# Left-factor remainders of an MLP matrix, made by ScalarE's negation and an accumulating transfer in 64 of 112 steps

## The chip, the cores and the metric

The kernel runs as one program on one core of a Trainium2 chip. The core has five engines that run side by side: TensorE (PE in the profile; its weight loads are PEld), VectorE (DVE), ScalarE (ACT), GpSimd (POOL) and SyncE (SP), which here only issues transfers. Sixteen DMA engines move data between the chip's memory (DRAM) and the core's on-chip memory (SBUF). Matmuls write to PSUM banks. The metric is the device time of one execution, in microseconds (us), median of three runs.

## The reference, cut to what matters

One layer of a diffusion backbone over 1024 tokens of width 1024, in fp32: a modulated RMSNorm, a convolution mixer and an mLSTM mixer, a merge and an output projection, and then an MLP with a squared ReLU. The change touches only the MLP's second matrix and the loads for the residual:

```python
def ffn(h, w1, w2):
    return jnp.square(jax.nn.relu(h @ w1)) @ w2
...
x = x + g1 * out
x = x + g2 * ffn(modulate(x, norm2_w[l], sh2, sc2), w_ff1[l], w_ff2[l])
...
return rmsnorm(x, final_norm_w)
```

`w_ff1` is 1024 x 4096 and `w_ff2` is 4096 x 1024. The result of the last line is the kernel's output.

## The kernel before, in words

**Precision.** Every large product is made from fp32 numbers that are cut in two. `split` has ScalarE write `hi`, the number in the matmul's rounded fp32r format, and VectorE write `lo = src - hi`, the remainder. A product then takes three matmul passes (`PASS`): hi by hi, hi by lo, lo by hi. In the third pass the left factor's `lo` is the weight that TensorE loads.

**The second matrix.** It is computed as seven products of half-size blocks (Strassen-Winograd), in the order m = 1, 5, 2, 6, 7, 3, 4. Each product has 512 tokens by 512 output columns, and its inner dimension of 2048 is walked in 16 steps k of 128, so that there are 7 x 16 = 112 steps (`steps`). One step is 4 token tiles x 3 passes = 12 matmuls of 128x512. For m = 4 the last token tile is cut in pieces of 288 and 224 columns. The last 4 steps of m = 4 are run tile by tile at the very end, with each tile's epilogue (gate, residual sum, RMSNorm, store) behind it.

**What a step needs.** The left factor is a 128x512 block of the squared-ReLU features or of a sum of their quarters. The first matrix's stage stores these to DRAM (`fq`) on POOL's queue. The right factor is a 128x512 block of `w_ff2`, or a sum that VectorE makes from several.

- `gather(i)` has SP load the left block to the left half `L` of a staging tile `wst` (six buffers) and the blocks of `w_ff2`. A right factor lies in the right half `R` of the same `wst` or in a page `wq`.
- `prepare(i)` splits both factors to `whi` and `wlo`, 128x1024 each, left half for the left factor. `ring` gives each of them four buffers, so step i + 4 writes where step i was read.
- `step(i, ...)` issues the 12 matmuls.

**Order.** Instructions of this stage are kept in program order on every engine. In iteration i of the main loop comes `gather(i + 4)`, then `prepare(i + 3)`, then the matmuls of step i, then a piece or two of pending VectorE work (`later`: sums of products in PSUM, gates, residuals). `prepare(i + 3)` overwrites the buffers of step i - 1, so ScalarE waits there until TensorE has finished step i - 1. A step's factors are thus made while TensorE runs the three steps ahead of it.

**How prepare splits before.** For m = 2, 7 and 4 both factors lie side by side in `wst` and are split as one 128x1024 piece. For m = 1, 5, 6 and 3 each half is split for itself, 128x512. `load_rows` loads the residual rows (eight tiles `x` of 512 KB, from `x1s` in DRAM): four at once at the start of m = 2, four at once within m = 6. `page` takes a 4 KB-per-partition buffer from a pool of 37; `keep` pins an instruction in program order.

Of the kernel before, what the change touches and what calls it, by code (L numbers as in the profile page):

```python
# [7 lines left out]
F32 = mybir.dt.float32  # L8
F32R = mybir.dt.float32r
AF = mybir.ActivationFunctionType  # L10
ALU = mybir.AluOpType
# [49 lines left out]
def tile_block(ctx: ExitStack, tc: tile.TileContext, x, cx, w_mod1, w_mod, w_v0, w_v, w_unit, w_conv, w_mls, w_o, w_f1, w_f2, cols_d, rows_d, cst_d, out):  # L61
    nc = tc.nc
# [19 lines left out]
    V, A, G, PE, SY = Engine(nc.vector), Engine(nc.scalar), Engine(nc.gpsimd), Engine(nc.tensor), nc.sync  # L82
# [10 lines left out]
    def dma(dst, src, pin=True):  # L93
        i = SY.dma_start(dst, src)
        if pin:
            tc.keep_in_program_order(i)
# [7 lines left out]
    def page(shape, dt=F32, name="pg"):  # L104
        return pg.tile(shape, dt, tag="pg", name=nm(name))
# [21 lines left out]
    def split(src, hi, lo, eng_hi=None, eng_lo=None, pin=False):  # L127
        p, pinned[0] = pinned[0], pinned[0] or pin
        V.tensor_copy(hi, src) if eng_hi is V else A.activation(hi, src, AF.Copy)
        (eng_lo or G).tensor_tensor(lo, src, hi.bitcast(F32), op=ALU.subtract)  # L130
        pinned[0] = p

    def load_w_now(src, eng_lo=None, eng_hi=None):
        n = 1024
        st = ws.tile([P, n], F32, tag="wst", name=nm("wst"))
        dma(st, src, pin=False)
        hi = ws.tile([P, n], F32R, tag="whi", name=nm("whi"))
        lo = ws.tile([P, n], F32R, tag="wlo", name=nm("wlo"))
        split(st, hi, lo, eng_hi, eng_lo)
        return hi, lo  # L140
# [32 lines left out]
    def keep(f):  # L173


        def call(*a, **kw):
            p, pinned[0] = pinned[0], True
            f(*a, **kw)
            pinned[0] = p

        return call
# [41 lines left out]
    def wide(st, eng_hi=None, eng_lo=None):  # L223
        hi, lo = page([P, 1024], F32R, "whi"), page([P, 1024], F32R, "wlo")
        split(st, hi, lo, eng_hi, eng_lo, pin=True)
        return hi, lo
# [573 lines left out]
    L, R = slice(0, 512), slice(512, 1024)  # L800
# [25 lines left out]
    def quads(name, n):  # L826

        return [dpool.tile([n, P, w], F32, name=f"{name}{i}") for i, w in enumerate((512, 1024, 1024, 1024))]
# [209 lines left out]
    def grow(s, bs):  # L1038
        g = page([P, D], name="grow")
        for hf in range(2):  # L1040
            for k in range(4):
                PE.transpose(bs[hf][:, k * P : (k + 1) * P], m2[:, s, 4 * hf + k : 4 * hf + k + 1].to_broadcast([P, P]), ident)
            A.copy(g[:, hf * 512 : hf * 512 + 512], bs[hf])
        return g
# [186 lines left out]
    def ring(n_, i, dt, n=4):  # L1231

        return home("2" + n_, i, n, lambda s_, d_, _: (in_ws if i % n < 2 else page)(s_, d_, n_), dt)
# [205 lines left out]
    fq = quads("fq", NP)  # L1439
# [128 lines left out]
    SRC = {1: (0, 0), 2: (1, 0), 4: (1, 1), 5: (2, 0), 6: (2, 1), 7: (3, 0), 3: (3, 1)}  # L1568
# [14 lines left out]
    steps = [(m, k) for m in (1, 5, 2, 6, 7, 3, 4) for k in range(NP)]  # L1583
    sums2, made2 = {}, {}

    def gather(i):

        m, k = steps[i]
        st = ring("wst", i, F32, 6)
        t_, h_ = SRC[m]  # L1590
        dma(st[:, L], fq[t_][k][:, h_ * 512 : h_ * 512 + 512])
        b = st[:, R]
        if m == 1:
            quarter(0, k)
            b = wblock(0, k)
        elif m == 5:
            quarter(1, k, b)
            V.tensor_tensor(wblock(0, k), b, wblock(0, k), op=ALU.subtract)
            b = wblock(0, k)
        elif m == 2:  # L1600
            quarter(2, k, b)
        elif m == 6:
            quarter(3, k)
            V.tensor_tensor(wblock(0, k), wblock(3, k), wblock(0, k), op=ALU.subtract)
            b = wblock(0, k)
        elif m == 7:
            quarter(1, k, b)
            V.tensor_tensor(b, wblock(3, k), b, op=ALU.subtract)
        elif m == 3:
            b = wblock(3, k)  # L1610
        else:
            quarter(2, k, b)
            V.tensor_tensor(b, b, wblock(0, k), op=ALU.subtract)
        sums2[i] = st, b

    def prepare(i):
        m, k = steps[i]
        st, b = sums2.pop(i)
        hi, lo = ring("whi", i, F32R), ring("wlo", i, F32R)
        if m in (2, 7, 4):  # L1620
            split(st, hi, lo, eng_lo=V)
        else:
            split(st[:, L], hi[:, L], lo[:, L], eng_lo=V)
            split(b, hi[:, R], lo[:, R], eng_lo=V)
        made2[i] = hi, lo

    def step(i, ts, o, more):
        m, k = steps[i]
        ab = made2[i]
        for j in ts:  # L1630
            for n_, (a, b) in enumerate(PASS):
                keep(PE.matmul)(o[j], ab[a][:, j * P : (j + 1) * P], ab[b][:, R], start=not more and k == 0 and n_ == 0, stop=k == NP - 1 and n_ == 2, skip_group_check=True)
# [5 lines left out]
    def last_tile(i, c):  # L1638
        m, k = steps[i]
        ab = made2[i]  # L1640
        cols_ = slice(512, 512 + CUT) if c == 0 else slice(512 + CUT, 1024)
        for n_, (a, b) in enumerate(PASS):
            keep(PE.matmul)(last_banks[c], ab[a][:, 3 * P : 4 * P], ab[b][:, cols_], start=k == 0 and n_ == 0, stop=k == NP - 1 and n_ == 2, skip_group_check=True)

    AHEAD = 3
    def four(name):
        t = [page2([P, 2, 512], name=name) for _ in range(2)]
        return [t[j // 2][:, j % 2, :] for j in range(4)]

    def gated_sum(t, s, o, u=None):  # L1650

        tmp = []

        def first():
            tmp.append(half("ftmp"))
            V.tensor_tensor(tmp[0], o, u if u is not None else g2[:, s], op=ALU.add if u is not None else ALU.mult)

        steps_ = [first]
        if u is not None:
            steps_.append(lambda: V.tensor_tensor(tmp[0], tmp[0], g2[:, s], op=ALU.mult))  # L1660
        steps_.append(lambda: V.tensor_tensor(x1[t][:, s], x1[t][:, s], tmp[0], op=ALU.add))
        return steps_

    def load_rows(ts):
        for t in ts:
            x1[t] = page([P, D], name="x1")
            dma(x1[t], x1s[t])
# [7 lines left out]
    def first_steps():  # L1675
# [2 lines left out]
            prepare(i)  # L1678
        gather(AHEAD)

    fp.steady(fe, first_steps)
    fp.end_d(NP - 1)

    LAST = 4
    tail = len(steps) - LAST
    assert not later
    for i in range(tail):
        m, k = steps[i]
        if i + AHEAD + 1 < len(steps):
            gather(i + AHEAD + 1)  # L1690
        prepare(i + AHEAD)
        o = Y if m in (5, 6, 3) else X
        if m == 4:
            step(i, range(3), o, True)
            for c in range(2):
                last_tile(i, c)
        else:
            step(i, range(4), o, m == 2)
        if i == 1:
            fp.post(NP - 1)  # L1700
            ua, ub = four("ua"), four("ub")
        if i == 3:
            g2 = grow(3, Y[0:2])
            fw = page([P, D], name="fw")
            dma(fw, rows_d[0:1, 1056:2080].to_broadcast([P, D]))
        if m == 2 and k == 0:
            load_rows(range(4))
        if m == 6 and k == 8:
            load_rows(range(4, 8))
        for _ in range(2 if m == 3 else 1):  # L1710
            if later:
                later.pop(0)()
        if k == NP - 1:
            assert not later
            if m == 1:
                for j in range(4):
                    A.copy(ua[j], X[j])
            elif m == 5:
                later += [lambda j=j: V.tensor_tensor(ub[j], Y[j], ua[j], op=ALU.add) for j in range(4)]
            elif m == 2:  # L1720
                for j in range(4):
                    later += gated_sum(j, L, X[j])
            elif m == 6:
                later += [lambda u=u, j=j: V.tensor_tensor(u[j], Y[j], u[j], op=ALU.add) for j in range(4) for u in (ua, ub)]
            elif m == 7:
                for j in range(4):
                    later += gated_sum(4 + j, R, X[j], ub[j])
                later += gated_sum(7, L, X[3], ua[3])
                for j in range(3):
                    later += gated_sum(4 + j, L, ua[j])  # L1730
            elif m == 3:
                a, b, c, d = [gated_sum(j, R, Y[j], ub[j]) for j in (2, 3, 0, 1)]
                a.pop(0)()
                b.pop(0)()
                later += a + b + c + d
    prepare(len(steps) - 1)
    for f in later:
        f()
# [124 lines left out]
```

## Time and profile before

| What | Value |
|---|---|
| median of three runs | 1784.93 us (1784.78 to 1785.35) |
| the profiled execution's own time | 1784.66 us |
| its span, first to last instruction | 1782.9 us |
| TensorE busy | 1738.9 us, 98% of the span |
| VectorE busy | 1269.6 us, 71% |
| ScalarE busy | 754.8 us, 42% |
| GpSimd busy | 192.8 us, 11% |
| moved by DMA | 261.11 MB, mean 146 GB/s |

The profile is one execution. All times in it count from the span's start. The span leaves out 1.8 us of the execution's own time, around the first and last instruction. A group's row gives the operation, its output and inputs by the program's names, the shape, a count, the busy time and the mean duration, and then the idle time of the engine just before, with what ended it. Nearly every instruction carries line 75 (a helper that records them), so groups are told apart by the names. A matmul's row of 386 to 390 ns is the time until its last result; the next one starts earlier, so the pace is read from the starts or from counts over a stretch. The second matrix's steps lie between 1450 and 1760 us, and the end of the span is the epilogue of the last four token tiles.

### The profile page before, as it was taken

The numbers are of one execution on the slowest core, as the hardware profiler recorded it, in microseconds if no ns is written. First come the engines' busy times: TensorE is split into PE (matmuls) and PEld (weight loads), VectorE is DVE, ScalarE is ACT, GpSimd is POOL, SyncE is SP. The second block draws the span as 40 slices with busy tenths as digits, with TensorE's granted clock in tenths as the row PEclk, the third lists the DMA queues.
The fourth block names the chain that finished last, engine by engine and source line by source line (L and its number), as shares of the span: only waits on it lengthen the run. The fifth ranks groups of instructions, "written<-read, shape, count | busy, mean of one in ns | idle before, by whom it ended". The sixth has DMA issues, their size and how long they took to land.

```text
span 1782.9 us, 23518 instructions
## 1 busy us (share of the span) xinstructions
PE 1738.9 (98%) x8633; PEld 1433.6 (80%) x8633; DVE 1269.6 (71%) x2224; ACT 754.8 (42%) x1239; POOL 192.8 (11%) x269
## 2 busy tenths in 40 slices
PE   7999999999999999999999999999999999999994
PEld 3898889877878888888888888877888888888884
DVE  5557565564876669878889987877666656577785
ACT  5633544556343332222244435644444354343434
POOL 3202122212300000000000001111011000000001
PEclk9999999999999999999999999999999999999997
DMA  8213131321534452433647255135334285665352
GB/s 325 77 47 91 46 93 43 89 70 61 174 145 142 157 197 97 140 131 124 228 167 284 71 207 183 72 138 187 130 141 178 112 279 194 233 230 199 104 181 94
DMA packets 102108, 261.11 MB, mean 146 GB/s; under 512 B 11624, under 2 KB 24808, under 8 KB 101992
## 3 DMA queue, kind: packets, MB, share of 16 engines
q1 hardware_dynamic: 85672, 200.88, 34.5%
q0 software_dynamic: 16320, 58.73, 8.3%
q8 instruction: 67, 1.10, 0.3%
q14 instruction: 49, 0.40, 0.1%
HBM read 198.62 MB, written 60.95 MB: 146 GB/s over the span
## 4 chain that ended last, share of the span: by engine, by line
PE 65%; DVE 4%; ACT 2%; issue 1%; ACTq 0%; DVEq 0%
PE psg L75 65%; ACT y L75 1%; DVE wlo L75 1%; DVE gate L75 0%; DVE wst L75 0%; ACT Fsh L75 0%; DVE y L75 0%; ACT fc L75 0%; DVE fc L75 0%; DVE Gv L75 0%; DVE x L75 0%; DVE ftmp L75 0%; DVE Ff L75 0%; DVE Fsl L75 0%; DVE u L75 0%
## 5 line engine op out<-in xcount | busy, mean ns | idle before, releaser
L75 DVE TENSOR_TENSOR wlo<-wst,whi 128x512 fp32r<-128x512 f32 (+1 forms) x236 | 223.5, 950 | 144.5 <-ACT whi L75 144.0
L75 ACT ACTIVATE whi<-wst 128x512 fp32r<-128x512 f32 (+1 forms) x238 | 195.8, 826 | 262.4 <-PE psg L75 170.4
L75 PE MATMUL psg<-whi,wlo 128*128 128x512 f32 (+2 forms) x688 | 266.2, 387 | 0.0
L75 PE MATMUL psg<-whi 128*128 128x512 f32 (+2 forms) x688 | 266.2, 387 | 0.0
L75 PE MATMUL psg<-wlo,whi 128*128 128x512 f32 (+2 forms) x688 | 265.7, 386 | 0.1
L75 PE MATMUL psg<-hh,whi 128*128 128x512 f32 x440 | 176.0, 406 | 0.0
L75 PE MATMUL psg<-hh,wlo 128*128 128x512 f32 x440 | 172.7, 398 | 1.3 <-DVE wlo L75 1.3
L75 PE MATMUL psg<-hl,whi 128*128 128x512 f32 x440 | 172.0, 397 | 0.0
L75 PEld LDWEIGHTS psg<-wlo,whi 128*128 128x128 f32 x688 | 129.3, 188 | 28.0 <-DVE wlo L75 0.6
L75 PEld LDWEIGHTS psg<-whi,wlo 128*128 128x128 f32 x688 | 129.2, 188 | 27.3
L75 PEld LDWEIGHTS psg<-whi 128*128 128x128 f32 x688 | 129.2, 188 | 27.0
L75 PEld LDWEIGHTS psg<-hh,wlo 128*128 128x128 f32 x440 | 83.1, 189 | 20.5 <-DVE wlo L75 1.7
L75 PEld LDWEIGHTS psg<-hl,whi 128*128 128x128 f32 x440 | 83.1, 189 | 17.3
L75 PEld LDWEIGHTS psg<-hh,whi 128*128 128x128 f32 x440 | 82.4, 189 | 17.9
L75 PE MATMUL psg<-oh,Fsl 128*128 128x512 f32 x240 | 94.8, 395 | 0.1
L75 PE MATMUL psg<-oh,Fsh 128*128 128x512 f32 x240 | 94.9, 395 | 0.0
L75 PE MATMUL psg<-ol,Fsh 128*128 128x512 f32 x240 | 94.5, 394 | 0.0
L75 DVE TENSOR_TENSOR u<-psg,u 128x512 f32<-128x512 f32 x67 | 45.8, 686 | 51.5 <-PE psg L75 51.5
L75 PE MATMUL psg<-whi,hh 128*128 128x256 f32 (+1 forms) x256 | 76.0, 297 | 0.0
L75 PE MATMUL psg<-wlo,hh 128*128 128x256 f32 (+1 forms) x256 | 73.2, 286 | 0.0
L75 PE MATMUL psg<-whi,hl 128*128 128x256 f32 (+1 forms) x256 | 73.1, 286 | 0.0
L75 POOL TENSOR_TENSOR wqz<-w,q 64x256 f32<-64x256 f32 x64 | 48.9, 768 | 159.1 <-PE pso L75 141.2
(347 smaller groups left out, 3868.3 us busy)
## 6 DMA issues: line engine op xcount, KB each, us to landing
wst<-fq SPq DMA_DIRECT2D x112, 256.0 KB, 2.8
wst<-in_w_unit_dram SPq DMA_DIRECT2D x38, 512.0 KB, 5.2
mst<-in_w_mod_dram SPq DMA_DIRECT2D x32, 512.0 KB, 4.3
fq<-Ff POOLq DMA_DIRECT2D x32, 512.0 KB, 4.2
wst<-in_w_f_dram SPq DMA_DIRECT2D x64, 256.0 KB, 3.1
wst<-in_w_f_dram SPq DMA_DIRECT2D x21, 512.0 KB, 4.3
Hwst<-in_w_unit_dram SPq DMA_DIRECT2D x18, 512.0 KB, 5.2
x<-in_x_dram SPq DMA_DIRECT2D x16, 512.0 KB, 6.0
```

Of the source, the lines that this page charges most:

```text
L75: i = f(*a, **kw)
```

## The change

For m = 5, 6, 7 and 3 (64 of the 112 steps) the left factor's `lo` no longer comes from VectorE. ScalarE writes `hi` as before and then `-hi` to `lo`, and a transfer issued from POOL's queue adds the left block from DRAM to `lo`, so that `lo = -hi + src`. The block is still loaded to `wst` as well, since `hi` is made from it. The right factor is split by ScalarE and VectorE as before, but now always as a piece of its own, so that m = 2 and m = 4 split two 128x512 halves in place of one 128x1024 piece. `load_rows` now loads one residual tile at k = 0, 3, 6, 9 of m = 2 and of m = 6. The two lines that set `LAST` and `tail` move up and are not used earlier.

```diff
+    def split_add(src, hi, lo, again):
+
+        keep(A.activation)(hi, src, AF.Copy)
+        keep(A.activation)(lo, hi.bitcast(F32), AF.Copy, scale=-1.0)
+        tc.keep_in_program_order(nc.gpsimd.dma_start(lo, again, accum_op=ALU.add))
...
         hi, lo = ring("whi", i, F32R), ring("wlo", i, F32R)
-        if m in (2, 7, 4):
-            split(st, hi, lo, eng_lo=V)
+        t_, h_ = SRC[m]
+        if m in (5, 6, 7, 3):
+            split_add(st[:, L], hi[:, L], lo[:, L], fq[t_][k][:, h_ * 512 : h_ * 512 + 512])
         else:
             split(st[:, L], hi[:, L], lo[:, L], eng_lo=V)
-            split(b, hi[:, R], lo[:, R], eng_lo=V)
+        split(b, hi[:, R], lo[:, R], eng_lo=V)
...
-        if m == 2 and k == 0:
-            load_rows(range(4))
-        if m == 6 and k == 8:
-            load_rows(range(4, 8))
+        if m in (2, 6) and k % 3 == 0 and k < 12:
+            load_rows((k // 3 + (0 if m == 2 else 4),))
```

How the order of instructions moves at four places. First ScalarE's rows where m = 5 begins (the four `whi` and `wlo` numbers are the four buffers of the ring, `wst` holds the left block and `wq` the right one):

```order
 L75 ACTIVATE whi_11617<-wst_11703 128x512
+L75 ACTIVATE wlo_11618<-whi_11617 128x512
 L75 ACTIVATE whi_11617<-wq_11615 128x512
 L75 ACTIVATE whi_11626<-wst_11725 128x512
+L75 ACTIVATE wlo_11627<-whi_11626 128x512
 L75 ACTIVATE whi_11626<-wq_11615 128x512
```

Between the two copies of each step stands the negation, and the copy of the right block comes one instruction later. At the same place VectorE's rows lose the left remainder of each step and keep the right one:

```order
 L75 TENSOR_TENSOR wq_11615<-wst_11725,wq_11615 128x512
-L75 TENSOR_TENSOR wlo_11618<-wst_11703,whi_11617 128x512
 L75 TENSOR_TENSOR wlo_11618<-wq_11615,whi_11617 128x512
 L75 TENSOR_TENSOR wq_11634<-wst_11613,wq_11634 128x512
-L75 TENSOR_TENSOR wlo_11627<-wst_11725,whi_11626 128x512
 L75 TENSOR_TENSOR wlo_11627<-wq_11615,whi_11626 128x512
```

On POOL's queue the accumulating transfers stand in a row of 64 between the first matrix's last stores and the epilogue (`xf` is a piece of the epilogue, `out_dram` the output; line 137 is the new function's). Before, and then after, where the first five of the 64 are shown:

```order
L91 DMA fq_8913<-Ff_1349_10058 128x1024
L91 DMA fq_8914<-Ff_1350_10059 128x1024
L75 TENSOR_TENSOR xf_13770<-x_1416_12794,fw_11802 128x512
L91 DMA out_dram<-y_13792 128x1024
L91 DMA out_dram<-y_13801 128x1024
```

```order
L91 DMA fq_8913<-Ff_1349_10058 128x1024
L91 DMA fq_8914<-Ff_1350_10059 128x1024
L137 DMA wlo_11618<-fq_8913 128x512
L137 DMA wlo_11627<-fq_8913 128x512
L137 DMA wlo_11637<-fq_8913 128x512
L137 DMA wlo_11708<-fq_8913 128x512
L137 DMA wlo_11618<-fq_8913 128x512
```

Nothing else is on that queue between the stores and the epilogue. Last, VectorE's rows for the last preparations of m = 4, before and then after (`x2` is two instructions, the left and the right half):

```order
L75 TENSOR_TENSOR wst_11642<-wst_11642,wq_11916 128x512
L75 TENSOR_TENSOR wlo_11637<-wst_11632,whi_11636 128x1024
L75 TENSOR_TENSOR wlo_11708<-wst_11642,whi_11707 128x1024
L75 TENSOR_SCALAR ss_1435_13771<-ss_1435_13771 128x1
L75 TENSOR_TENSOR ftmp_13787<-psg_5424,grow_11791 128x512
```

```order
L75 TENSOR_TENSOR wst_11642<-wst_11642,wq_11916 128x512
L75 TENSOR_TENSOR wlo_11637<-wst_11632,whi_11636 128x512 x2
L75 TENSOR_TENSOR wlo_11708<-wst_11642,whi_11707 128x512 x2
L75 TENSOR_SCALAR ss_1435_13931<-ss_1435_13931 128x1
L75 TENSOR_TENSOR ftmp_13947<-psg_5424,grow_11791 128x512
```

The order is the same; each piece of 1024 columns has become two of 512. ScalarE's copies to `whi` are cut in the same way there. TensorE's instructions keep their order; in the 64 steps the first matmul that uses the left `lo` now also waits for the transfer.

More of the change, by code (lines that the diff above doesn't have):

```diff
@@ L1679, in first_steps @@
         gather(AHEAD)
+    LAST = 4
+    tail = len(steps) - LAST
     fp.steady(fe, first_steps)
     fp.end_d(NP - 1)
-    LAST = 4
-    tail = len(steps) - LAST
     assert not later
```

## The prediction

> **What bounds the kernel now.** I read the page's busy line first, then the stretches of the five products around the change, then the waits of TensorE there, and last the final matmuls.
>
> ```profile
> span 1782.9 us, 23518 instructions
> PE 1738.9 (98%) x8633; PEld 1433.6 (80%) x8633; DVE 1269.6 (71%) x2224; ACT 754.8 (42%) x1239; POOL 192.8 (11%) x269
> ```
>
> TensorE is busy for 98% of the span, VectorE for 71%. That is an average, so the stretches of m = 5, 2, 6, 7 and 3 follow, one row each (16 steps of 12 matmuls):
>
> ```profile
> core 0: us, PE busy (x) PEld busy (x) DVE busy (x) ACT busy (x) POOL busy (x), PEclk, DMA share, GB/s
> 1494.60:1538.70 44.10, 44.10 (x194) 36.08 (x193) 27.11 (x40) 18.83 (x31) 0.00 (x0) 1.00 0.68 232
> 1538.70:1582.70 44.00, 44.00 (x193) 36.05 (x192) 25.23 (x28) 17.25 (x19) 0.00 (x0) 1.00 0.61 198
> 1582.70:1626.70 44.00, 44.00 (x193) 36.03 (x192) 34.49 (x53) 18.18 (x29) 0.00 (x0) 1.00 0.69 238
> 1626.70:1670.80 44.10, 44.10 (x194) 36.07 (x194) 31.64 (x39) 17.30 (x20) 0.00 (x0) 1.00 0.45 146
> 1670.80:1714.80 44.00, 44.00 (x193) 36.03 (x192) 36.53 (x55) 18.14 (x29) 1.29 (x1) 1.00 0.44 142
> ```
>
> TensorE is never idle in them, at a granted clock of 1.00. 192 matmuls, and one or two cut by a stretch's edges, take 44.0 us, whether VectorE works 25 or 37 us beside them and whether DMA moves 142 or 238 GB/s. So a matmul is paced at 0.23 us and a step at 2.75 us, and relief of VectorE there is worth nothing. From 1450 to 1752 us TensorE and its loads have one wait in all, and SP waits for VectorE to free staging buffers:
>
> ```profile
> PEld psg L75 <- DVE wlo L75: 0.6, 1, 0.6
> ...
> SPq L94 <- DVE wlo L75: 194.7, 102, 8.9
> ```
>
> **The engines' work.** The prices are the mean durations of the same shapes in the stretch from 1450 to 1750 us.
>
> ```profile
> L75 ACT ACTIVATE whi<-wst 128x1024 fp32r<-128x1024 f32 x48 | 50.9, 1061 | 82.2 <-PE psg L75 63.3 <-issue 5.4 <-DMA wq<-in_w_f_dram 5.1
> L75 ACT ACTIVATE whi<-wst 128x512 fp32r<-128x512 f32 x61 | 38.5, 632 | 88.1 <-issue 46.5 <-PE psg L75 40.7 <-ACT whi L75 0.9
> L75 DVE TENSOR_TENSOR wlo<-wst,whi 128x1024 fp32r<-128x1024 f32 x48 | 58.8, 1225 | 42.7 <-ACT whi L75 42.7
> L75 DVE TENSOR_TENSOR wlo<-wst,whi 128x512 fp32r<-128x512 f32 x61 | 42.7, 700 | 46.5 <-ACT whi L75 46.2
> ```
>
> VectorE: m = 5, 6 and 3 lose 48 subtractions of 0.700 us, -33.6 us. m = 7 goes from one of 1.225 to one of 0.700 us in 16 steps, -8.4. m = 2 and 4 go from 1.225 to two of 0.700 in 32 steps, +5.6. In all it does 36 us less. ScalarE: 48 negations priced as the copy of that shape, +30.3 us; m = 7 three of 0.632 for one of 1.061, +13.4; m = 2 and 4 two for one, +6.5; in all +50. In a changed step it works 3 x 0.632 = 1.9 us of 2.75. Both stay below TensorE's pace, so both terms are 0 on the path. What covers them is the 44.0 us of matmuls per product, and the cover ends only where a factor comes late.
>
> **When the new remainder must land.** ScalarE's rows in m = 5 show when a preparation starts, and two rows of the epilogue how soon POOL follows its releaser:
>
> ```profile
> 1500.14 0.63 ACT L75 ACTIVATE whi<-wst 128x512 fp32r<-128x512 f32 x1 [1.57 <-issue]
> 1500.67 0.62 ACT L75 ACTIVATE whi<-wq 128x512 fp32r<-128x512 f32 x1
> 1502.91 0.63 ACT L75 ACTIVATE whi<-wst 128x512 fp32r<-128x512 f32 x1 [1.62 <-issue]
> ...
> 1755.60 1.28 DVE L75 SCALAR_TENSOR_TENSOR y<-x,rs,fw 128x1024 f32<-128x1024 f32 x1
> 1757.18 0.59 POOL L91 DMA_DIRECT2D out_dram<-y  x1 [79.71 <-DVE rs L75]
> ```
>
> Preparations start 2.77 us apart, one step, since each waits for the buffers of the step that TensorE has just finished. The step prepared comes three steps later, and its left remainder is wanted as the weight of the third matmul, loaded one matmul ahead: 3 x 2.75 + 0.23 = 8.5 us after the start. Of this the copy and the negation take 0.63 + 0.62, and POOL issues 0.3 us after its releaser ended (1755.60 + 1.28 = 1756.88 to 1757.18). That leaves 8.5 - 1.55 = 6.9 us from the issue of the accumulating transfer to its landing. POOL itself is busy 0.59 us per issue there, a fifth of a step, and nothing else is on its queue until the epilogue, so no store is held up.
>
> No accumulating transfer is in the trace of before. The nearest rows are plain ones: POOL's stores in the stretch from 1200 to 1500 us (512 and 256 KB), then all transfers from or to `fq` (minimum, median, maximum) and the residual rows, 512 KB each, four in the queue at once.
>
> ```profile
> fq<-Ff POOLq DMA_DIRECT2D x29, 512.0 KB, 4.2
> fq<-Ffc POOLq DMA_DIRECT2D x13, 256.0 KB, 2.3
> ...
> DMA to landing us min/median/max: 2.3/2.9/8.7
> ...
> DMA to landing us min/median/max: 5.3/6.9/8.8
> ```
>
> The ends are 2.3 us (the same 256 KB from the same queue, as if adding cost nothing) and 8.8 us (the slowest of the residual rows). I take 4.2 us, the 512 KB store from the same queue, since a transfer that also reads its destination handles twice the bytes it lands. It would land 2.7 us early, at a cost of 0. Where it lands later than 6.9 us, the four-buffer ring closes a loop: each us late holds TensorE, whose next finish starts the next preparation, and one turn of the loop is four steps. So each us beyond 6.9 costs 0.25 us per step, 16 us over 64 steps.
>
> **What the DMA engines must carry.** Two stretches of 8 and 16 us show the most that the engines moved, and what the end of m = 1 takes with m = 5's first loads and no residual rows; below them are the issues of the left block (whole span) and of a block of `w_ff2` in the crowded 1590 to 1610 us:
>
> ```profile
> 1531.00:1539.00 8.00, 8.00 (x37) 6.51 (x36) 3.68 (x3) 2.94 (x4) 0.00 (x0) 1.00 1.00 386
> 1478.00:1494.00 16.00, 16.00 (x72) 13.04 (x71) 10.31 (x17) 7.87 (x14) 0.00 (x0) 1.00 0.61 196
> ...
> wst<-fq SPq DMA_DIRECT2D x112, 256.0 KB, 2.8
> ...
> wq<-in_w_f_dram SPq DMA_DIRECT2D x5, 256.0 KB, 6.7
> ```
>
> The added 256 KB (262 kB) per step of 2.75 us are 95 GB/s: 196 + 95 = 291 of 386 GB/s if they weigh as plain bytes, 387 if they weigh double. Plain is well hidden; double just fills the engines. A short excess is covered too: a left block's load for step n + 6 goes out when preparation n has read its buffer, about 2 us into it, so it has some 6 x 2.75 - 2 = 14.5 us, and needs 2.8 us, or 6.7 in a crowd: about 8 us to spare (an estimate from these rows). The residual rows, now one per three steps, spread over 25 us what came in one burst. TensorE did not stall in that burst either (44.00 of 44.00 us above), so this edit is 0.
>
> The Trainium skill has a rule that speaks against the change: its page "Collectives: The Full Stack", section "The bandwidth ceiling: the fold count and why AG ≠ RS ≠ AR", says that an add inside a DMA engine reads two sources for each chunk that it writes and so runs at half a copy's rate. That is the double weight, and by it the engines would be full at 387 of 386 GB/s and the sum would still be 0 to a few us, by the spare time; no run here shows an accumulating transfer yet.
>
> **The last preparation.** The one stall of TensorE is on the chain that ends last; under its rows stand the two matmuls from TensorE's timeline:
>
> ```profile
> 1748.67 1.07 ACT whi L75
> 1749.74 0.02 issue
> 1749.77 1.24 DVE wlo L75
> 1751.00 0.04 issue
> 1751.04 0.75 PE psg L75 x2
> ...
> 1750.51 0.40 PE L75 MATMUL psg<-whi 128*128 128x512 f32 x1
> 1751.04 0.51 PE L75 MATMUL psg<-wlo,whi 128*128 128x512 f32 x1
> ```
>
> The matmul after 1750.51 was due 0.23 us later, at 1750.74, and began at 1751.04: 0.30 us of stall. Now ScalarE's halves start at 1748.67 and 0.53 us later (the spacing of the two copies above), and end by 1749.82. VectorE subtracts the left half beside the second copy and the right one from 1749.95 to 1750.65, ahead of 1750.74. So the stall goes, -0.3 us, and the epilogue, which hangs on this first tile, moves up with it. What is late next is TensorE itself.
>
> **Sum.** VectorE 0, ScalarE 0, transfers 0, rows 0, last preparation -0.3 us: the profiled execution's own 1784.66 (span 1782.9 and 1.8 around it) becomes 1784.4. It stands 0.27 us below the median of the runs, so against the median I say 1784.6. About 0.2% (3.6 us) is what a measurement of this kernel can tell from no change.
>
> **Rivals.**
>
> *The remainder lands late* (slower). For it: the residual rows take 6.9 us when the queue is full, and the sixteen engines would be at 75 to 100% of what they ever moved. Against it: the same queue's 256 KB take 2.3 us. It decides from 7.1 us on; at 8.8 us it costs 16 x 1.9 = 30 us, 1815 us; at 7.9 us 16 us, 1801. Chance 0.18.
>
> *The DMA engines become the bound* (slower). An added byte that weighs threefold makes 196 + 286 = 482 of 386 GB/s, a step of 3.44 us instead of 2.75. In m = 5 the excess of 11 us meets 8 us to spare; in m = 6 and 7 22 us, and 5 us for four residual rows, meet 8 us again; m = 3 loads no block of `w_ff2` and recovers. That is 3 + 19 = 22 us, 1807 us. For it speaks only that the operation is unknown; against it that double still fits. Chance 0.10.
>
> *POOL paces the steps* (slower). If writing out such a transfer took POOL longer than a step, say 3.5 us, 64 x 0.75 = 48 us, 1833 us. Its rows say 0.59. Chance 0.05.
>
> *VectorE's relief shows* (faster). At most its 36 us would come off, 1748 us. Against it stand five stretches of 44.0 us with different loads of VectorE. Chance 0.02.
>
> **How the numbers follow.** My forecast has the rest, 0.65: 1784.6 us, its own range 1783.8 to 1788. Slower by over 0.2% is 0.18 + 0.10 + 0.05 = 0.33, faster 0.02, the same 0.65. Leaving out about half of the slower cases takes the range up to 1802; below, 1783.5 takes in the last preparation's 0.3 us twice over and the runs' own spread.
>
> **What the changed profile would show.** Right: the five stretches at 44.0 us with TensorE busy throughout, no wait of TensorE for a transfer to `wlo`, these transfers landing in 2.3 to 6.9 us, VectorE some 36 us lighter and ScalarE 50 us heavier, and no gap before the last step's second matmul. Wrong: waits of TensorE for `wlo<-fq`, spread evenly over all 64 steps if the landing is late, or growing through m = 5 and through m = 6 and 7 with a DMA share of 1.00 if the engines are full; or POOL's rows of `wlo<-fq` longer than 2.75 us each. Most would go wrong at the one operation that no row shows, the accumulating transfer.

## The result, and the profile after

The changed kernel takes 1788.56 us (median of 13 runs, 1786.59 to 1789.27), the kernel before, measured beside it, 1784.93 us (1784.19 to 1785.35). The ratio is 1.0019, 95% interval 1.0012 to 1.0027: slower by 3.6 us, where 1784.6 us was forecast. The changed kernel's profiled execution took 1788.26 us with a span of 1786.5 us, 3.6 us longer than before.

The page of the changed kernel: the span, the engines, the two DMA queues (q1 is SP's, q0 POOL's; packets, MB, share of 16 engines), the issue of the new transfer on POOL, and two issue rows whose last column is the median time to landing.

```profile
span 1786.5 us, 23806 instructions
PE 1737.8 (97%) x8633; PEld 1432.2 (80%) x8633; DVE 1233.8 (69%) x2208; ACT 800.3 (45%) x1351; POOL 248.2 (14%) x333
...
q1 hardware_dynamic: 85672, 200.88, 34.6%
q0 software_dynamic: 25536, 75.51, 13.8%
...
L137 POOL DMA_DIRECT2D wlo<-fq x64 | 56.0, 876 | 194.5 <-ACT wlo L75 190.0
...
wst<-fq SPq DMA_DIRECT2D x112, 256.0 KB, 4.4
...
wlo<-fq POOLq DMA_DIRECT2D x64, 256.0 KB, 6.2
```

VectorE lost 35.8 us of work (1269.6 to 1233.8) and ScalarE gained 45.5; TensorE has 1 us less busy time in a longer span, so it waits. The new transfer lands in 6.2 us at the median, and the plain load of the same left block now takes 4.4 us where it took 2.8. The waits of TensorE for transfers between 1440 and 1752 us, and then the landing of all 64 new transfers:

```profile
PEld psg L75 <- DMA wlo<-fq: 3.9, 4, 1.2
...
PE psg L75 <- DMA wlo<-fq: 2.2, 4, 0.7
...
DMA to landing us min/median/max: 4.0/6.2/8.0
```

Four weight loads wait, and with each the matmul that it serves (the two rows overlap in time). TensorE's timeline names the four matmuls; in brackets is its idle time and what ended it:

```profile
1504.60 0.50 PE L75 MATMUL psg<-whi,wlo 128*128 128x512 f32 x1 [0.64 <-DMA wlo<-fq]
...
1534.77 0.39 PE L75 MATMUL psg<-wlo,whi 128*128 128x512 f32 x1
1535.90 0.50 PE L75 MATMUL psg<-whi,wlo 128*128 128x512 f32 x1 [0.75 <-DMA wlo<-fq]
1536.24 0.40 PE L75 MATMUL psg<-whi 128*128 128x512 f32 x1
...
1588.99 0.50 PE L75 MATMUL psg<-whi,wlo 128*128 128x512 f32 x1 [0.52 <-DMA wlo<-fq]
...
1600.69 0.50 PE L75 MATMUL psg<-whi,wlo 128*128 128x512 f32 x1 [0.32 <-DMA wlo<-fq]
```

Each is the first third-pass matmul of a step, the one that loads the left `lo`. It starts 1.03, 1.13, 0.91 and 0.71 us after the matmul ahead of it, where the pace is 0.23 us, and the next one is 0.11 us late too (1535.90 to 1536.24). Matmul by matmul against the trace of before, the delay grows by 0.96, 1.01, 0.84 and 0.74 us at these four places and just behind them, 3.55 us in all. (The expectations below divide the same sum as 1.0, 0.94, 0.91 and 0.70.) The delay was already 0.44 us when m = 5 began, 0.32 of it from the first 42 us of the span, far ahead of the change, and it falls by 0.41 us at the last preparation. 3.55 + 0.44 - 0.41 = 3.58 us, the difference of the spans. But for those two other terms, which nearly cancel, the loss sits in four matmuls out of the 768 of the changed steps.

What stands behind the second of them, from the timelines of POOL and of SP's queue:

```profile
1527.87 0.88 POOL L137 DMA_DIRECT2D wlo<-fq  x1 [1.90 <-ACT wlo L75]
...
1527.89 0.46 SPq L94 DMA_DIRECT2D x<-x1s  x1
```

The transfer of step m = 5, k = 14 and the first residual row (512 KB) are issued 0.02 us apart. The transfer lands 8.0 us after its issue, at 1535.87, and the matmul starts at 1535.90. The third and fourth gaps have the same neighbour: their transfers, issued at 1581.14 and 1592.97, have residual rows issued at 1581.15 and at 1589.38, and the last of these rows lands only at 1598.81. The first gap (step m = 5, k = 3) has no residual row near it. Its cause is on ScalarE:

```profile
1494.02 2.03 ACT L75 COPY ua<-psg 128x512 f32<-128x512 f32 x4
1495.92 0.66 ACT L75 ACTIVATE whi<-wst 128x512 fp32r<-128x512 f32 x1
1496.61 0.64 ACT L75 ACTIVATE wlo<-whi 128x512 fp32r<-128x512 f32 x1
```

Four copies of finished sums out of PSUM (`ua`) stand ahead of that preparation. ScalarE starts it at 1495.92, 3.63 us behind the preparation ahead (1492.29) instead of 2.75, so the transfer is issued 0.9 us late, at 1497.54, and lands 7.02 us later.

Last, the busy time for m = 5, moved by the delay up to there, and for 44 us within m = 6:

```profile
core 0: us, PE busy (x) PEld busy (x) DVE busy (x) ACT busy (x) POOL busy (x), PEclk, DMA share, GB/s
1494.96:1539.06 44.10, 42.72 (x186) 34.35 (x185) 18.79 (x30) 27.30 (x48) 11.36 (x13) 1.00 1.05 285
...
1586.14:1630.14 44.00, 43.16 (x187) 34.57 (x186) 24.58 (x39) 27.61 (x47) 13.75 (x16) 1.00 1.09 304
```

At the same clock of 1.00, 186 or 187 matmuls fit where 193 or 194 did. The DMA share was 0.68 and 0.69 there and is 1.05 and 1.09 (the share adds up the packets' own times, which overlap).

### The profile page after: what moved, and what is told of

Same layout as the page of the kernel before. It is cut to its first block, busy times and chain, and to the rows that moved or that the text cites. A ratio compares the mean times of both kernels' runs of the same rounds, so it can differ in the third digit from the quotient of the medians.

```text
span 1786.5 us, 23806 instructions
## 1 busy us (share of the span) xinstructions
PE 1737.8 (97%) x8633; PEld 1432.2 (80%) x8633; DVE 1233.8 (69%) x2208; ACT 800.3 (45%) x1351; POOL 248.2 (14%) x333
## 3 DMA queue, kind: packets, MB, share of 16 engines
q0 software_dynamic: 25536, 75.51, 13.8%
## 4 chain that ended last, share of the span: by engine, by line
PE 60%; issue 5%; DVE 3%; ACT 2%; POOL 1%; DMA 0%; POOLq 0%; ACTq 0%; DVEq 0%
PE psg L75 60%; POOL wlo L137 1%; ACT y L75 1%; DMA wlo<-fq 0%; DVE wst L75 0%; ACT Fsh L75 0%; DVE y L75 0%; ACT fc L75 0%; DVE fc L75 0%; DVE x L75 0%; DVE ftmp L75 0%; DVE Ff L75 0%; DVE Fsl L75 0%; DVE ol L75 0%; DVE f L75 0%
## 5 line engine op out<-in xcount | busy, mean ns | idle before, releaser
L75 ACT ACTIVATE whi<-wst 128x512 fp32r<-128x512 f32 (+1 forms) x286 | 202.1, 720 | 218.5 <-PE psg L75 162.6
L75 DVE TENSOR_TENSOR wlo<-wst,whi 128x512 fp32r<-128x512 f32 (+1 forms) x220 | 183.5, 850 | 113.2 <-ACT whi L75 112.9
L75 DVE TENSOR_TENSOR wlo<-wq,whi 128x512 fp32r<-128x512 f32 x64 | 46.0, 719 | 65.2 <-ACT whi L75 62.9
L137 POOL DMA_DIRECT2D wlo<-fq x64 | 56.0, 876 | 194.5 <-ACT wlo L75 190.0
```

The source lines that it names most:

```text
L75: i = f(*a, **kw)
L137: tc.keep_in_program_order(nc.gpsimd.dma_start(lo, again, accum_op=ALU.add))
```

## The experiments

Three theories stood against each other. A: the loss is the lateness of single remainders, at the residual rows and behind the four copies, and nothing else. B: the added instructions, waits and POOL's issues cost by themselves. C: the DMA engines, full through m = 5, 6 and 7, cost by the sum of their bytes. The kernel before took 1784.76 us beside the first four runs, 1784.72 beside the next four and 1784.55 beside the last. Ratios are to it.

**The transfer without its addition.**

```diff
-        tc.keep_in_program_order(nc.gpsimd.dma_start(lo, again, accum_op=ALU.add))
+        tc.keep_in_program_order(nc.gpsimd.dma_start(lo, again))
```

> The changed kernel, but the transfer from POOL's queue copies the left block to lo in place of adding it to the negated hi (the addition is left out; every instruction, wait and byte landed stays). Theory A (the adding transfer lands later than the 6.9 us it has, at four places): a copied 256 KB lands in about 3 us, TensorE has no wait for wlo<-fq, and the time is 1784.6 to 1785.3 us. Rival B (the cost is in what the change adds beside the transfer's duration: ScalarE's third instruction, TensorE's extra wait, the halves): stays at 1788 to 1789 us with the gaps where they were.

Measured: 1785.20 us, ratio 1.0003 (0.9994 to 1.0011). The issue on POOL, the landing, the one wait left, and POOL's queue:

```profile
L137 POOL DMA_DIRECT2D wlo<-fq x64: 537/537/542, 1488.1 to 1705.9; - x64
...
DMA to landing us min/median/max: 3.1/4.3/7.3
...
PEld psg L75 <- DMA wlo<-fq: 0.4, 1, 0.4
...
q0 software_dynamic: 25536, 75.51, 11.7%
```

Instructions, waits, issues and bytes are all still there, and the loss is not, so B falls. The addition is what makes the transfers too late. (POOL's issue got shorter too, from 0.876 to 0.537 us, but 0.34 us off the slowest landing of 8.0 would leave 7.7, still over 6.9.) q0 went from 16320 to 25536 packets; its share rose from 8.3% to 11.7% of 16 x 1783 us with the plain transfer and to 13.8% with the adding one: 970 and 1577 us for 9216 packets, or 0.105 and 0.171 us each, by the packets' own recorded times, which overlap. The rule of the Trainium skill that the prediction cited ("Collectives: The Full Stack", section "The bandwidth ceiling: the fold count and why AG ≠ RS ≠ AR") is given there for ReduceScatter against AllGather; carried over to this transfer, it would double the time. The trace agrees in the direction and gives 1.6 times. The packets' records also divide the landing: the first packet of an adding transfer starts 2.7 us after its issue at the median, and its last one ends 2.7 us behind that; with the plain transfer it is 1.7 and 2.1 us. So waiting to begin takes as long as moving, and it grew by more: 1.0 us, of which POOL's issue is 0.3. Even the plain transfer takes 4.3 us here, where about 3 were expected, and 7.3 beside a residual row, so the 2.3 us of POOL's stores was never to be had in these products.

**The residual rows where no such transfer is under way.** The eight rows are loaded one per step at m = 2, k = 4 to 11.

```diff
-        if m in (2, 6) and k % 3 == 0 and k < 12:
-            load_rows((k // 3 + (0 if m == 2 else 4),))
+        if m == 2 and 4 <= k < 12:
+            load_rows((k - 4,))
```

> The changed kernel with all eight residual rows loaded at k = 4 to 11 of m = 2, when no adding transfer is under way. Theory A: three of the four gaps of TensorE (0.94, 0.91 and 0.70 us, each beside a residual row) go and the one at 1504.6 us stays: 1788.6 - 2.6 = 1786.0 us. Rival C (the DMA engines are full all through m = 5, 6 and 7, rows or not): gaps remain in m = 5 and m = 6, 1788 us or little below.

Measured: 1785.97 us, ratio 1.0006 (0.9997 to 1.0015). The waits of TensorE that are left all belong to the first gap, at 1504 us, and to the step behind it:

```profile
PEld psg L75 <- DMA wlo<-fq: 1.6, 2, 1.4
...
PE psg L75 <- DMA wlo<-fq: 1.0, 1, 1.0
```

The other three gaps are gone with the rows. By the packets' records, the transfers of those three steps (m = 5, k = 14; m = 6, k = 1 and 5) began to move 4.0 to 4.1 us after their issue in the changed kernel and 2.4 to 3.1 us after it here. A row makes the transfer late by its start, then; why the start waits that long, no run tells.

**Step m = 5, k = 3 by VectorE.** `if m in (5, 6, 7, 3) and (m, k) != (5, 3)` selects the new way for 63 steps.

> The changed kernel, but the left remainder of one step (m = 5, k = 3, the one prepared behind ScalarE's four copies of the first product) is made by VectorE as before. Theory A: the gap at 1504.6 us (1.0 us with its after-effect) goes, the others stay: 1787.6 us. Rival C: no change beyond noise, 1788.5 us, the gap comes a step later.

Measured: 1787.61 us, ratio 1.0017 (1.0008 to 1.0026). The first gap is gone, those at the rows stay, and in m = 7 a new one stands at 1630.6 us, where a matmul starts 0.88 us after the one ahead of it, with no residual row beside it. The time alone decides nothing, since the interval reaches from 1786.2 to 1789.4 us and so holds the 1788.5 of C too; the trace shows that the first gap did not move a step on. That the time agrees with theory A to 0.01 us is luck, for it hides two things: the first 42 us ran 0.24 us shorter than in the changed kernel's profile, and the new gap. From m = 6, k = 9 to m = 7, k = 6 of the changed kernel the remainders land only 0.1 to 0.4 us ahead of their weight loads, so a gap can also open where nothing in the program marks the place.

**Both edits.**

> Both edits: residual rows within m = 2, and step m = 5, k = 3 by VectorE. Theory A: no gap is left, only the 0.3 us gain at the last preparation stays: 1784.6 us, a little below the kernel before. Rival C: 1787 us or more with gaps in m = 6. Rival B: 1788 us.

Measured: 1784.61 us, ratio 0.9999 (0.9990 to 1.0008). No wait of TensorE for a transfer is left, and the slowest landing is under the budget of 6.9 us, while the engines stay full (m = 5 and m = 6):

```profile
DMA to landing us min/median/max: 4.2/5.6/6.6
...
1494.60:1538.70 44.10, 44.10 (x194) 36.10 (x194) 20.49 (x32) 26.94 (x47) 10.46 (x12) 1.00 1.01 273
...
1582.70:1626.70 44.00, 44.00 (x193) 36.08 (x192) 25.48 (x41) 28.56 (x48) 13.96 (x16) 1.00 1.07 285
```

A DMA share of 1.01 and 1.07 costs TensorE nothing as long as each transfer lands in time. C falls as a cost of its own; its part is that full engines leave the landings little room.

**The copies instead of the step.** The rows as above, and the four `ua` copies by VectorE; all 64 transfers stay.

```diff
-                    A.copy(ua[j], X[j])
+                    V.tensor_copy(ua[j], X[j])
```

> The changed kernel with the eight residual rows loaded one per step at m = 2, k = 4 to 11, where no accumulating transfer is under way, and with the four copies ua (quarters of the token tiles' sums, which ScalarE made ahead of the preparation of step m = 5, k = 3) made by VectorE. All 64 accumulating transfers stay. Theory A: the gap at m = 5, k = 3 came from the transfer's issue 0.9 us late behind those copies, so it goes too, and with it the last gap: 1784.6 us. If that gap came from the DMA engines at that moment alone, it stays: 1785.7 to 1786.0 us, as with the rows' edit alone.

Measured: 1784.85 us, ratio 1.0000 (0.9991 to 1.0009), no wait of TensorE for a transfer:

```profile
DMA to landing us min/median/max: 4.1/5.7/6.8
...
1493.50 0.87 POOL L137 DMA_DIRECT2D wlo<-fq  x1 [1.88 <-ACT wlo L75]
1496.29 0.86 POOL L137 DMA_DIRECT2D wlo<-fq  x1 [1.92 <-ACT wlo L75]
1499.02 0.86 POOL L137 DMA_DIRECT2D wlo<-fq  x1 [1.86 <-ACT wlo L75]
```

The issues are back at one per step, and the first gap is gone. The late issue was thus the cause, by two ways that no run separates: with the copies on ScalarE (and the rows moved) that transfer was issued 0.9 us late and also took 7.36 us, with the next one only 1.86 us behind it; without them it took 5.94 us.

**Five buffers instead of four.** `ring("whi", i, F32R, 5)`, the same for `wlo`, and `AHEAD = 4`: each preparation comes one step earlier.

> The changed kernel with five buffers for each split factor instead of four, and each preparation one step earlier (four steps ahead of its use), so that a remainder has 2.75 us more to land, 9.7 us in place of 6.9. Rows, bytes and instructions stay. Theory A: the slowest landing of the changed kernel was 8.0 us, so no gap is left, TensorE runs its five products at 44.0 us each and the time is that of the kernel before, 1784.6 us (if the factors' places in SBUF leave the matmuls' pace alone). Theory C: the bytes are the same, so 1788.5 us.

Measured: 1784.88 us, ratio 1.0001 (0.9992 to 1.0010). Rows and copies are as in the changed kernel, and the landings are even slower, yet TensorE waits for none:

```profile
DMA to landing us min/median/max: 4.2/6.7/8.4
...
1494.60:1538.70 44.10, 44.10 (x194) 36.13 (x193) 20.19 (x32) 27.25 (x47) 10.46 (x12) 1.00 1.03 288
```

It is not the landing time that costs, but its excess over the budget, as theory A says.

**A smaller budget.** The negation is done twice, so that each transfer is issued 0.63 us later.

```diff
         keep(A.activation)(lo, hi.bitcast(F32), AF.Copy, scale=-1.0)
+        keep(A.activation)(lo, hi.bitcast(F32), AF.Copy, scale=-1.0)
```

> The changed kernel with ScalarE's negation done twice in each of the 64 steps, so that every accumulating transfer is issued 0.63 us later; bytes and transfers are the same. Theory A: the budget from issue to landing falls from 6.9 to 6.3 us, below the median landing of 6.2 us in the crowded products. The four gaps grow by up to 0.63 us each (2.5 us), and the steps from m = 6, k = 6 to m = 7, k = 6, whose remainders landed 0.1 to 0.5 us ahead of the weight load, are late by 0.1 to 0.5 us; by the four-step loop one step in four pays that, some 1.5 to 2 us. In all 4 to 5 us more, 1791.5 to 1794 us. A theory that the gaps come from ScalarE or POOL being busy alone, or from bytes alone, gives 1788.5 us: ScalarE has 0.2 us of a step left and POOL 1.9.

Measured: 1791.73 us, ratio 1.0038 (1.0025 to 1.0050): 7.0 us over before, where the changed kernel had 3.6. The landings are no slower, but 11 weight loads wait instead of 4:

```profile
DMA to landing us min/median/max: 3.9/5.7/7.9
...
PEld psg L75 <- DMA wlo<-fq: 8.7, 11, 1.7
```

The 0.63 us on one engine, idle enough to hold it, cost 3.4 us. The time is within the range expected, at its low end, but the difference is below the 4 to 5 us it was made from. A reason may be that each wait also delays the issues behind it and gives the DMA engines a rest; no run shows that by itself.

**The burst of residual rows.** `load_rows` as in the kernel before, four rows at m = 2, k = 0 and four at m = 6, k = 8.

> The changed kernel with the residual rows loaded again as in the kernel before, four at once at the start of m = 2 and four at once within m = 6. Theory A (a remainder that lands after its weight load is due costs just its lateness, and what makes it late is what lies in the DMA engines ahead of it): four rows are 2 MB, 5.4 us at 386 GB/s, where one row is 1.4 us, so the transfers issued around each burst land in some 11 to 13 us; fewer places with a gap, but of 2 to 5 us each, the one at m = 5, k = 3 unchanged, and in all 1791 to 1796 us. The step of my prediction that priced the rows' edit at 0 would then be wrong for another reason than its sign: spreading the rows saves time once the transfers are there. Theory C (the added traffic costs by its sum): the same bytes move, so as the changed kernel, 1788.5 us.

Measured: 1789.66 us, ratio 1.0028 (1.0018 to 1.0038): 4.9 us over before.

```profile
DMA to landing us min/median/max: 4.1/6.3/8.7
...
PEld psg L75 <- DMA wlo<-fq: 5.3, 5, 1.9
```

The direction is that of theory A, the size is not: no transfer took 11 to 13 us. Four rows queued at once thus did not all go ahead of the transfer; at m = 5, k = 14 it landed in 8.7 us where it took 8.0 beside one row. There are four gaps again, one of them at 1631.8 us in m = 7, again without a row. Spreading the rows was worth some 1.3 us (4.9 less 3.6), but this is not firm: the intervals of the two ratios, 1.0018 to 1.0038 and 1.0012 to 1.0027, overlap. Moving them is worth some 2.4 us (3.6 less 1.2).

**The cut halves alone.** `if False:` in place of the new way's condition: VectorE makes all remainders, the rows stay spread.

> The changed kernel without its negations and accumulating transfers: VectorE makes the left remainder in all 112 steps. What is left of the change is that m = 2, 7 and 4 split two 128x512 halves instead of one 128x1024 piece, and that the residual rows come one per three steps. Theory A: no remainder comes by a transfer, so no gap at the rows and none at m = 5, k = 3; the stall of 0.30 us ahead of the last step's second matmul goes, as the cut alone does that: before less 0.3 us, 1784.5 us, and the span some 0.3 us shorter than before's 1782.9. If the spread rows cost by themselves, there are waits of TensorE between 1450 and 1752 us here too; if the stall's end hung on VectorE's relief and not on the cut, the matmul after 1750.5 us still comes 0.53 us behind the one ahead of it.

Measured: 1784.14 us, ratio 0.9997 (0.9988 to 1.0006), span 1782.0 us. The last stall, from TensorE's timeline:

```profile
1750.01 0.40 PE L75 MATMUL psg<-whi 128*128 128x512 f32 x1
1750.24 0.40 PE L75 MATMUL psg<-wlo,whi 128*128 128x512 f32 x1
...
1750.70 0.39 PE L75 MATMUL psg<-whi 128*128 128x512 f32 x1
1750.93 0.39 PE L75 MATMUL psg<-wlo,whi 128*128 128x512 f32 x1
```

Every second-pass matmul follows 0.23 us behind its first; the one at 0.53 us is gone, as it is in the changed kernel. Here the relief of VectorE is left out, and the run with the burst of rows, which has the cut too, loses the stall as well, so it is the cut that does it. The delay falls by 0.41 us there: 0.30 of the stall, and 0.11 of the matmul behind it. TensorE has no wait for a transfer here, so the spread rows cost nothing without the adding transfers. This is the lowest median of all, 0.4 us under before, which the interval can't tell from nothing; of the 0.9 us that its profiled span is shorter, 0.5 lie ahead of m = 5, where nothing was changed; no version beats the kernel before measurably.

## Why the prediction was wrong, step by step

- **The landing, taken at 4.2 us: wrong, and with it the sign.** It measured 4.0 to 8.0 us, median 6.2, so that the 2.7 us to spare became 0.7 at the median and a lack of 1.1 at the worst. The bounds of 2.3 and 8.8 us held it, and the choice between them, the 512 KB store "from the same queue", was the wrong row. That store ran at other times, when the DMA engines were emptier (a share of 0.48 from 1200 to 1500 us, against 1.05 and 1.09 here). In the crowd where this transfer runs, the prediction had rows of 6.7 us (256 KB of `w_ff2`) and 6.9 us (residual rows), and these were the near ones.
- **"The residual rows ... so this edit is 0": wrong.** Three of the four gaps stand at these rows and go with them: 2.6 us of delay in the trace, and 2.4 by the medians (3.6 over before against 1.2). It is their place beside the new transfers that costs and not their spreading, since four at once lost no less. The proof offered, that TensorE did not stall in the burst before, was no proof: before, no remainder came through the DMA engines. That a left block's load has "about 8 us to spare" was right and answered for another transfer; the accumulating one had 0.7 us at its median.
- **"Preparations start 2.77 us apart": right but for one step.** At m = 5, k = 3 the four `ua` copies push the start back by 0.9 us. They stand in the program before the change too and cost nothing there; they were not looked for. One gap, 1.0 us.
- **The budget of 6.9 us: right.** The weight load behind the matmul at 1534.77 was due then, one matmul ahead, 6.90 us after the issue at 1527.87. The other steps that stand behind no gap have 6.9 to 7.0 us as well, but for k = 4 of m = 3. Its issue came 0.7 us late, for a reason that no row shows, and cost nothing, since the transfer landed in 4.0 us there. With 2.75 us more the loss went, as that sum says; with 0.63 us less it grew, by less than was expected.
- **The rival "the remainder lands late": the right mechanism, with too high a price.** Its 0.25 us per step holds for a landing that is late in all steps. Here 13 of the 64 took 7.0 us or more (five in m = 5, and k = 1 to 8 of m = 6), and only four of them made TensorE wait: the three steps behind each gap had been put back with it and had 7.6 to 7.9 us. That is the loop of four steps that the prediction described. The step that opens a gap pays its lateness whole, 0.7 to 1.0 us with the 0.11 us of the next matmul.
- **The double weight and the full engines: nearly right.** 291 to 387 of 386 GB/s was the forecast; 285 and 304 GB/s were moved, with a share above 1.00, in m = 5 and 6. That this costs nothing by itself held, by the run with both edits.
- **The terms of 0 for VectorE and ScalarE, and POOL's pace: right.** -35.8 us for -36, +45.5 for +50, and 0.876 us per issue for 0.59, under a third of a step. Neither relief nor load showed.
- **The last preparation, -0.3 us: right in its cause, a little small.** The delay falls by 0.41 us, in the changed kernel and with the cut alone; the 0.11 us of the matmul behind the stall was left out.

## What to carry to other kernels

When a value comes to take a longer way, compare its budget with the slowest landing in the crowd in which it will run, not with a median from a quieter place: with 6.9 us against 6.2 at the median and 8.0 at the worst, everything that issues a large transfer at that moment, or delays the issue, can cost. Whatever was hidden before (a load of 512 KB, four copies) must be asked again whether it still is, since its cover belonged to the old way. And VectorE, lighter by 36 us beside a full TensorE, gave nothing back in any run here, so this trade could at best come out even.

## What was not expected of the hardware

- The issue of an adding transfer held POOL for 0.876 us, that of the same transfer without the addition for 0.537 us.
- A packet of the adding transfer was recorded with 0.171 us, that of a plain one from the same queue 0.105 us, and the plain loads beside them slowed from 2.8 to 4.4 us (3.5 with the plain transfer).
- A DMA share above 1.00 for 44 us cost TensorE nothing, while a single 512 KB load could make a transfer late, by holding back its first packet.
